# A planner that knows ScalarE's table loads and has own constants for two halves of the program, 128-row opening matmuls, and evictions shared between engines, in a hybrid encoder layer

## The chip, the cores and the metric

The kernel runs on one core of a Trainium2 chip. The metric is device time in microseconds (us), from the start of the program to its end. The time before is the median of three runs, 1055.0 us (1053.02 to 1058.98). The core has five engines that run their own instruction streams: PE (TensorE, matmuls), DVE (VectorE), ACT (ScalarE), POOL (GpSimd), and SP (SyncE, which here only issues transfers). They wait for each other through semaphores.

## The reference

One layer of an encoder over `x` of shape (1, 512, 1024), in float32. All constants below are fixed: 32 SSD heads of 64 in 8 groups, state 128, chunks of 128 tokens; 16 query heads and 4 key/value heads of 64; a feed-forward width of 4096.

```python
h = rmsnorm(x, pre_mix_norm)
z, xbc, dt_raw, q, k, v, gates = split_cols(h @ w_in, IN_SPLITS)      # w_in: 1024 x 9792
y_ssd  = ssd_branch(z, xbc, dt_raw, ...)      # conv of 5 taps, silu, scan in both directions, gated norm, @ w_ssd_out
y_attn = window_attention(q, k, v, attn_sink, rel_bias_table) @ w_attn_out     # +-128 tokens
g = sigmoid(gates + b_gate)
mixed = (g_ssd * y_ssd + g_attn * y_attn) @ w_o
x = x + rmsnorm(mixed, post_mix_norm)
h = rmsnorm(x, pre_mlp_norm)
f = square(relu(h @ w_mlp_in)) @ w_mlp_out    # 1024 x 4096 and 4096 x 1024
x = x + rmsnorm(f, post_mlp_norm)
```

The scan of one group and direction takes, for each chunk of 128 tokens, the product of the group's C and B (a 128x128 matrix), decays it, multiplies it with the chunk's inputs, and adds what the state carries over from the chunks before; the state itself is a product of B (transposed) with the weighed inputs.

## The kernel before, in words

**Numbers.** A large float32 operand is split into a rounded high part `hi` and the rest `lo`, both in the type fp32r, and a product is done as three matmuls into one accumulator: hi*hi, hi*lo, lo*hi (`mm3`). Each weight of 128x1024 thus needs a cast for its high part (ACT: line 585 in the in-projection, 1783 in the MLP) and a subtraction for its low part (lines 589 and 1792). Strings of letters say who subtracts: "v" is DVE, "p" POOL in quarters, "d" ACT and an adding DMA of POOL. The w_o product and the MLP are done by Strassen's scheme: seven products of half-size blocks, so the operands are also sums of blocks (`sums`, line 1671; `fold2`, line 1737). Small operands (`split`, lines 532 and 533) are cast on ACT and subtracted on DVE.

**Stages, by the trace's times.** Opening (0 to 25 us, `start`): load x, spread the norm weights over all partitions, norm, transpose and split the first 256 tokens' activations, and project to `v` and `dt`. Then the in-projection in column chunks of 128 with the scan of the eight groups and the attention heads worked in between (25 to about 690 us); the mix with w_o (to about 722); `norm_rows`, `flip_h2` (line 1630: the normed rows are transposed by 32 PE transposes, 16 for each half of the tokens, and scaled by the norm weight as they leave PSUM, line 1648) and the MLP's operands; the MLP's four up-projections U0 to U3 and four down-projections D0 to D3 (to 1041), and the closing norm (to 1054).

**The scan around the change.** For a group, the conv of B ends on ACT, its transpose goes through DRAM (the tile `pd`, written and read by SP, lines 1009 and 1012), the result is weighed, cast to `bth` (line 532) with a rest `btl`, also named `bth` in the profile (line 533), and then multiplied with the chunks' inputs `xh` on PE. Between the matmuls that make B and those that use `bth`, PE has other columns of the in-projection to work on: matmuls `pp<-b,wh` of 512 columns.

**The order.** The program is first written down in the order of Python, quantum by quantum. `Planner` (line 171) then simulates the five engines with a cost for every instruction, chooses for each engine the next instruction of those that are ready in the simulation, and `chain` (line 620) fixes the resulting order of every engine by dependencies. Matmuls are taken in program order, except that `next_matmul` (line 214) prefers those whose operands have been ready for some spare time (`SPARE_TIME`, by the engine that makes them), and holds the present kind of matmul (fp32r, fp32, or 64 rows wide) for up to `HOLD` ns before it changes kind; before `EARLY` ns of simulated time the hold is off. The other engines take what is due first (`deadlines`, with `DUE`), and wait for a more urgent instruction if it comes within `WAIT` of its cost. `LONGER` is a factor on costs, `TAIL` and `LEAD` belong to a transfer. The order is thus a result of all costs together, and a new constant anywhere may move instructions everywhere behind it.

**The opening's clock.** The first instructions of PE are six products of a zero tile (`WARM`), whose results nobody reads; then `self.gb`, two products of a row of ones (1x128) with the norm weights (1x512), which spread these over the partitions.

Of the kernel before, what the change touches and what calls it, by code (L numbers as in the profile page):

```python
# [29 lines left out]
LO_EARLY = "pppp"  # L30
LO_LATE = "vvpp"
# [4 lines left out]
DEFER, DEFER_BY = (3, 5), 9  # L36
WARM2 = 0
EARLY = 20000
NORM2 = 1, 0, 1
LO_V = "pvpvpvpv"  # L40
# [4 lines left out]
FETCH, STAGE = 2, 1  # L45
# [3 lines left out]
DUE = 7000  # L49
FAR = 2  # L50
LO_UP = "vdvp"
LO_DN = "vpvvvv"
RELU = "aaaaaa"
ADDS = "vvvhh"
LO_F = (), ()
LO_END = "dv"
FLIP = 2
# [113 lines left out]
class Planner:  # L171
# [8 lines left out]
    HOLD = 4000  # L180
# [4 lines left out]
    def __init__(self, instructions, tags, held=()):  # L185
        names = {"PE": "PE", "DVE": "DVE", "Activation": "ACT", "Pool": "POOL", "SP": "SP"}
        self.ins = [i for i in instructions if type(i).__name__ != "BassTilePoolBoundary"]
        self.eng = [names[str(i.engine).split(".")[-1]] for i in self.ins]
        self.tags = tags
        self.depend()  # L190
        last = None
        for n, i in enumerate(self.ins):
            if self.eng[n] == "PE":
                last = n
            elif i.name in held:
                self.turn[n].add(last)
                self.next[last].append(n)
        self.cost = [self.duration(n) for n in range(len(self.ins))]
        self.kind = [self.matmul_kind(n) if e == "PE" else None for n, e in enumerate(self.eng)]

# [11 lines left out]
    SPARE_TIME = {"SP": 3000, "POOL": 500, "DVE": 500, "ACT": 500, "PE": 0}  # L212

    def next_matmul(self, some, ready, soft, t, kind):
# [9 lines left out]
        held = lambda n: ready[n] + (0 if t < EARLY else 2 if self.ins[n].is_transpose else 1) * self.HOLD  # L224
# [134 lines left out]
    TAIL = 1400  # L359
    LONGER = 1.02  # L360
# [8 lines left out]
    WAIT = 0.2  # L369

    def plan(self):
        wait = self.WAIT
# [10 lines left out]
        queue, kind, landed = 0.0, None, []  # L383
        order, self.when = {e: [] for e in self.OVERLAP}, {}
        for _ in self.ins:
# [6 lines left out]
            t, e = best  # L392
            some = avail[e]
# [11 lines left out]
            c *= (2 if t < self.COLD else 1) if e == "PE" else self.LONGER  # L405
            end = t + c
            if e == "SP":
                queue = max(queue, t + self.LEAD) + self.transfer(n)
                free[e], end = end, queue + self.TAIL
# [10 lines left out]
            else:  # L420
# [5 lines left out]
                end += 2500 if "DMA" in type(self.ins[n]).__name__ else 0  # L426
            for s in self.post[n]:
                same = self.eng[s] == e == "PE"
                ready[s] = max(ready[s], free[e] if same else end + self.AFTER[self.eng[s]])
                if self.eng[s] == "PE":  # L430
                    soft[s] = max(soft[s], ready[s] + self.SPARE_TIME[e])
                left[s] -= 1
                if not left[s]:
                    avail[self.eng[s]].append(s)
# [17 lines left out]
class Trunk:  # L452
# [215 lines left out]
    def start(self):  # L668
# [4 lines left out]
        g = [get("g") for _ in range(2)]  # L673
        for j in range(2):
# [6 lines left out]
        self.zero, one = get("zero", (128, 128)), get("one", (128, 128))  # L681
        nc.vector.memset(self.zero, 0.0)
# [30 lines left out]
        for j in range(2):  # L713
            self.mm(self.gb[j], one[:1], g[j][:1], True, True)
# [769 lines left out]
    def mix_second(self, k):  # L1484
# [15 lines left out]
        self.mheld.extend([{"S1": p}, {"S4": q}, {"A22": (c,)}])  # L1500
# [129 lines left out]
    def flip_h2(self, t2):  # L1630
# [28 lines left out]
    def operand_h(self, a, r, parts=1):  # L1659
# [6 lines left out]
        for i in range(parts):  # L1666
            c = slice(i * 1024 // parts, (i + 1) * 1024 // parts)
            self.split(hi[:, c], lo[:, c], r[:, c])
# [169 lines left out]
    def up_quanta(self, p, banks):  # L1838
# [10 lines left out]

        return self.fold2(src, self.hops, banks, self.up_done(p), LO_UP, after, True)  # L1850

# [82 lines left out]
    def down_quanta(self, part, banks):  # L1934
# [17 lines left out]
        return self.fold2(src, self.fops[part], banks, done, LO_END if part == 3 else LO_DN, lambda a: self.give(*self.fops[part].pop(a)), False, part == 3)  # L1952
# [127 lines left out]
```

## Time and profile before

| what | value |
|---|---|
| median of three runs | 1055.0 us (1053.02 to 1058.98) |
| the profiled execution | 1055.77 us, of which the span of the instructions is 1054.0 us |
| mean granted clock of PE over the span | 0.994 |
| PE busy | 1033.5 us, 98% of the span, 5808 records |
| DVE, ACT, POOL busy | 862.9, 694.7 and 689.6 us (82, 66 and 65%) |
| in the MLP, 722 to 1041 us: PE, DVE | 315.8 and 290.9 of 319 us busy |

In the profile's rows a line number is that of the code above, `out<-in` are the program's names with the buffer numbers left out, `128*128` the rows and columns of the array in use, and "[2.75 <-ACT bth L532]" says that the engine stood idle for 2.75 us just before, and that an instruction of ACT, on tile `bth`, line 532, ended that. A matmul with three fp32r products has three instructions; an fp32 matmul of the code has several records (two products of 1x512 are four records in the opening). Matmul records overlap in time, since the array is a pipeline; what one costs is the distance to the next one's start. PE's clock is granted by a throttle: in the stretches of a table by windows, PEclk is the share of the full speed.

### The profile page before, as it was taken

The page shows a single profiled execution, that of the slowest core. Times are in us where ns is not written, and L with a number is a line of the kernel's source. Part 1 is how long each engine was busy: PE and PEld are TensorE (multiplying, and loading weights), DVE is VectorE, ACT ScalarE, POOL GpSimd, SP SyncE. Part 2 cuts the span into 40 slices and gives each one's busy share as a digit, 9 for nine tenths or more (in the row PEclk, how much of TensorE's full clock was granted, in tenths as well). Part 3 has the DMA queues.
Part 4 walks back from the last instruction along what each step waited for, and adds up shares of the span by engine and source line. Part 5 has one row for each costly group of instructions (what it writes and reads, how often), then busy time and mean ns, then how long its engine had stood idle before and what let it go on. Part 6 is the DMA issues. An engine that isn't in the chain of part 4 may idle for free. (4 is left out here: it accounts for less than half of the span.)

```text
span 1054.0 us, 17140 instructions
## 1 busy us (share of the span) xinstructions
PE 1033.5 (98%) x5808; PEld 889.1 (84%) x5808; DVE 862.9 (82%) x1237; ACT 694.7 (66%) x1293; POOL 689.6 (65%) x784
## 2 busy tenths in 40 slices
PE   9999899999999999999999999999999999999996
PEld 7888788888888888887888888888999998998885
DVE  5668788787896986696988775779988989969998
ACT  4577778768776664755676423578975864856863
POOL 3556659667869988998989767548853554254410
PEclk9999999999999999999999999999999999999998
DMA  7439968979999776758682499676784754855953
GB/s 226 116 103 266 256 177 250 245 187 261 249 219 242 227 191 178 190 160 218 166 216 76 145 305 343 190 223 217 197 201 101 223 142 98 219 138 143 278 142 100
DMA packets 232424, 206.24 MB, mean 196 GB/s; under 512 B 15341, under 2 KB 185557, under 8 KB 232336
## 3 DMA queue, kind: packets, MB, share of 16 engines
q1 hardware_dynamic: 225068, 185.68, 61.9%
q0 software_dynamic: 7120, 19.40, 10.4%
q8 instruction: 46, 0.75, 0.3%
q14 instruction: 42, 0.34, 0.1%
q10 hardware_dynamic: 148, 0.07, 0.0%
HBM read 163.35 MB, written 29.69 MB: 183 GB/s over the span
## 5 line engine op out<-in xcount | busy, mean ns | idle before, releaser
L515 PE MATMUL pp<-b,wh 128*128 128x512 f32 (+1 forms) x1424 | 431.2, 384 | 2.0 <-DVE b L533 1.5
L589 POOL TENSOR_TENSOR wl<-wr,wh 128x256 fp32r<-128x256 f32 (+1 forms) x365 | 308.3, 871 | 110.7 <-ACT wh L585 81.2
L515 PEld LDWEIGHTS pp<-b,wh 128*128 128x128 f32 x1424 | 262.8, 189 | 53.8 <-DVE b L533 1.9
L515 PE MATMUL pp<-b,wl 128*128 128x512 f32 (+1 forms) x712 | 272.8, 384 | 0.0
L515 PEld LDWEIGHTS pp<-b,wl 128*128 128x128 f32 x712 | 134.4, 189 | 25.8 <-issue 0.3
L585 ACT CAST wh<-wr 128x1024 fp32r<-128x1024 f32 (+1 forms) x99 | 102.7, 1039 | 50.3 <-POOL wl L589 32.6
L1783 ACT CAST wh<-wd 128x1024 fp32r<-128x1024 f32 x63 | 65.2, 1050 | 19.3 <-PE ps L515 6.6
L1792 DVE TENSOR_TENSOR wl<-wd,wh 128x1024 fp32r<-128x1024 f32 x46 | 65.9, 1444 | 8.2 <-ACT wh L1783 6.7
L515 PE MATMUL ps<-b,wh 128*128 128x256 f32 x400 | 72.0, 283 | 0.0
L515 PE MATMUL pp<-wh,fh 128*128 128x512 f32 x176 | 68.9, 392 | 0.8 <-ACT fh L1699 0.6
L515 PE MATMUL pp<-wl,fh 128*128 128x512 f32 x176 | 68.9, 391 | 0.2 <-DVE wl L1792 0.2
L515 PE MATMUL pp<-wh,fl 128*128 128x512 f32 x176 | 67.8, 390 | 0.0
L515 PEld LDWEIGHTS ps<-b,wh 128*128 128x128 f32 x400 | 62.3, 191 | 0.9
L515 PE MATMUL ps<-b,wl 128*128 128x256 f32 x200 | 55.7, 284 | 0.0
L1792 POOL TENSOR_TENSOR wl<-carved,wh 128x256 fp32r<-128x256 f32 x32 | 40.0, 1294 | 14.1 <-ACT wh L1783 7.2
L1792 POOL TENSOR_TENSOR wl<-wd,wh 128x256 fp32r<-128x256 f32 x24 | 35.5, 1504 | 19.4 <-ACT wh L1783 17.8
L1783 ACT CAST wh<-carved 128x1024 fp32r<-128x1024 f32 x34 | 35.4, 1049 | 19.0 <-DVE carved L1744 10.8
L515 PE MATMUL ps<-sh,wh 128*128 128x256 f32 x160 | 45.3, 283 | 0.0
L515 PE MATMUL ps<-sh,wl 128*128 128x256 f32 x160 | 45.2, 283 | 0.0
L515 PE MATMUL ps<-sl,wh 128*128 128x256 f32 x160 | 45.2, 283 | 0.0
L1788 POOL DMA_DIRECT2D wl<-carved x11 | 9.9, 901 | 48.8 <-ACT wl L1787 38.4
L515 PEld LDWEIGHTS pp<-wh,fh 128*128 128x128 f32 x176 | 33.1, 188 | 7.8 <-ACT fh L1699 0.8
(968 smaller groups left out, 2636.9 us busy)
## 6 DMA issues: line engine op xcount, KB each, us to landing
wr<-in_w_in SPq DMA_DIRECT2D x74, 512.0 KB, 5.7
wd<-in_w_mlp_out SPq DMA_DIRECT2D x26, 512.0 KB, 5.7
wd<-in_w_mlp_in SPq DMA_DIRECT2D x22, 512.0 KB, 5.4
pd<-t SPq DMA_DIRECT2D x16, 640.0 KB, 6.0
pT<-pd SPq DMA_DIRECT2D x64, 160.0 KB, 5.7
wr<-in_w_ssd_out SPq DMA_DIRECT2D x14, 512.0 KB, 4.4
rf<-csT SPq DMA_DIRECT2D x27, 256.0 KB, 5.6
wl<-carved POOLq DMA_DIRECT2D x11, 512.0 KB, 6.1
```

Of the source, the lines that this page charges most:

```text
L515: self.nc.tensor.matmul(out, lhsT, rhs, start=start, stop=stop, skip_group_check=more)
L585: self.nc.scalar.copy(hi[:, :m], raw)
L589: engines[e].tensor_tensor(lo[:, c], raw[:, c], hi[:, c].bitcast(F32), op=ALU.subtract)
L1783: nc.scalar.copy(hi, w)
L1788: nc.gpsimd.dma_start(low, w, accum_op=ALU.add)
L1792: (nc.vector if e == "v" else nc.gpsimd).tensor_tensor(low[:, q], w[:, q], hi[:, q].bitcast(F32), op=ALU.subtract)
```

## The change

1. **The planner** adds 1283 ns to the simulated cost of an instruction of ACT whose activation table is another than the last one's (`table_of`: Ln and Sqrt each their own, Exp and Tanh together). Its constants `HOLD`, `SPARE_SP`, `SPARE_VEC`, `TAIL`, `LONGER` and `WAIT` have a value for the scan and one for what follows `ENTRY` = 690000 ns of simulated time (`HOLD` a third one from 30 us later). `HOLD` becomes 8000, 500, 4000 (was 4000), the spare time for a transfer's result 1000 and 3000 (was 3000), that for a vector engine's 500 and 800 (was 500), `TAIL` 1600 and 1400 (was 1400); `WAIT` and `LONGER` keep their values. `EARLY` goes from 20 to 80 us and `DUE` from 7000 to 6000.
2. **The opening** fills `g` and `one` with zeros on all 128 rows, so that the products that spread the norm weights are 128 rows deep. The identity's transfer is issued ahead of those of `g`, which wait for the zeros. `WARM2` adds two products of the zero tile; the order puts them beside the six that were there. The low parts of the opening's weights are all subtracted on DVE (`LO_V`).
3. **Shares.** Low parts: the gates' weights (`LO_EARLY`, `LO_LATE`) and, of the weights of the first two up-projections, the fourth of every four (`LO_UP`) go from POOL to DVE. Half of the 16 evictions behind the PE transposes of `flip_h2` go from ACT to DVE (`EVICT_H`), and the first relu and square of each up-projection become one instruction of DVE (`RELU`).
4. **Places.** `FLIP` 2 to 1, `FETCH` 2 to 1, `DEFER` without quantum 5, and `mix_second` holds the block sum `q` one product longer.

Counted over both programs: DVE does 6 more low parts of 128x1024 in the MLP, 4 more instructions of 128x512 (relu), 8 more of 128x256 (evictions), 24 more low parts of 128x256 in the gates, 4 more of 128x320 and two more fills; POOL does 24 fewer pieces of 128x256 in the MLP, 24 fewer in the gates and 4 fewer of 128x320; ACT does 8 fewer instructions of 128x512 and 8 fewer of 128x256; PE has two more 128x128 products. ACT's table loads are four in both programs, ahead of the same instructions (lines 735, 892, 990 and 1960).

```diff
-LO_EARLY = "pppp"
-LO_LATE = "vvpp"
+LO_EARLY = "vvpp"
+LO_LATE = "vvvp"
-DEFER, DEFER_BY = (3, 5), 9
-WARM2 = 0
-EARLY = 20000
+DEFER, DEFER_BY = (3,), 9
+WARM2 = 2
+EARLY = 80000
-LO_V = "pvpvpvpv"
+LO_V = "vvvvvvvv"
-FETCH, STAGE = 2, 1
+FETCH, STAGE = 1, 1
-DUE = 7000
+DUE = 6000
-LO_UP = "vdvp"
+LO_UP = "vdvv", "vdvv", "vdvp", "vdvp"
+EVICT_H = "av", "av"
-RELU = "aaaaaa"
+RELU = "vaaaaa"
-FLIP = 2
+FLIP = 1
...
-    HOLD = 4000
+    ENTRY = 690000
+    HOLD = 8000, 500, 4000
...
+    @staticmethod
+    def table_of(i):
+        f = str(getattr(i, "func", "")).split(".")[-1]
+        return f if f in ("Ln", "Sqrt") else "Exp" if f in ("Exp", "Tanh") else None
...
-    SPARE_TIME = {"SP": 3000, "POOL": 500, "DVE": 500, "ACT": 500, "PE": 0}
+    SPARE_SP = 1000, 3000
+    SPARE_VEC = 500, 800
...
+        hold = self.HOLD[(t > self.ENTRY) + (t > self.ENTRY + 30000)]
...
-    TAIL = 1400
+    TAIL = 1600, 1400
+    TABLE = 1283
...
+            if e == "ACT" and self.table[n] not in (None, table):
+                c, table = c + self.TABLE * (table is not None), self.table[n]
...
         g = [get("g") for _ in range(2)]
+        self.zero, one = get("zero", (128, 128)), get("one", (128, 128))
+        nc.vector.memset(self.zero, 0.0)
+        nc.vector.memset(g[0], 0.0)
+        nc.gpsimd.memset(g[1], 0.0)
         for j in range(2):
             nc.scalar.dma_start(g[j][:1], self.d_pre_mix_norm[0:1, j * 512:(j + 1) * 512])
...
-        self.zero, one = get("zero", (128, 128)), get("one", (128, 128))
-        nc.vector.memset(self.zero, 0.0)
+        nc.vector.memset(one, 0.0)
         nc.vector.memset(one[:1], 1.0)
...
-            self.mm(self.gb[j], one[:1], g[j][:1], True, True)
+            self.mm(self.gb[j], one, g[j], True, True)
...
-        self.mheld.extend([{"S1": p}, {"S4": q}, {"A22": (c,)}])
+        self.mheld.extend([{"S1": p}, {"S3": q}, {"A22": (c,)}])
...
                 for i in range(2):
-                    nc.scalar.activation(r[:, (k + i) * 256:(k + i + 1) * 256], ps[:, i * 256:(i + 1) * 256], AF.Copy,
-                                         scale=self.g3(4 * kh + k + i))
+                    dst, src, g = r[:, (k + i) * 256:(k + i + 1) * 256], ps[:, i * 256:(i + 1) * 256], self.g3(4 * kh + k + i)
+                    if EVICT_H[t2][(4 * kh + k + i) % len(EVICT_H[t2])] == "a":
+                        nc.scalar.activation(dst, src, AF.Copy, scale=g)
+                    else:
+                        nc.vector.tensor_scalar(dst, src, g, None, op0=ALU.mult)
```

**The order at three places.** In the rows, the numbers behind a name tell tiles apart and differ between the two programs; "x3" is three instructions in a row.

PE at the states of scan group 0 (about 111 us in the trace). `pp_1300` (after: `pp_1305`) is a column chunk of the in-projection with 24 matmuls of 512 columns, `C,bt` the products of C and B, and `xh,bth` the state products. Before:

```order
L515 MATMUL pp_1300<-b_143,wh_1101 128x512
L515 MATMUL pp_1300<-b_145,wh_1101 128x512
L515 MATMUL pp_1300<-b_143,wl_1102 128x512
L515 MATMUL pp_1300<-b_143,wh_1101 128x512
L515 MATMUL pp_1300<-b_145,wh_1101 128x512
L515 MATMUL ps_1273<-C_1093,bt_927 128x128 x2
L515 MATMUL ps_1278<-xh_1122,bth_1118 128x256 x2
```

After:

```order
L532 MATMUL pp_1305<-b_149,wl_1107 128x512
L532 MATMUL pp_1305<-b_149,wh_1106 128x512
L532 MATMUL pp_1305<-b_151,wh_1106 128x512
L532 MATMUL ps_1278<-C_1098,bt_932 128x128 x2
L532 MATMUL ps_1283<-xh_1127,bth_1123 128x256 x3
L532 MATMUL ps_1288<-xh_1127,bth_1123 128x256 x3
L532 MATMUL pp_1305<-b_149,wl_1107 128x512
```

Before, five matmuls of the chunk stand ahead of the state products and 19 behind them; now 23 stand ahead and one behind.

ACT at the same place: the cast of `bth` and what stands ahead of it (`rf` are decays of the scan, line 1266, and `P` softmax numerators, line 990, 997). Before:

```order
L997 ACTIVATE E_1029<-E_1029,sm_1048 128x256
L997 ACTIVATE P_1066<-P_1066,sm_1048 128x256
L585 CAST wh_1255<-wr_1108 128x1024
L1266 ACTIVATE rf_1026<-rf_1026,tables_403 128x128 x3
L990 ACTIVATE P_1202,sm_1197<-P_1202,mx_1196 128x384
L532 CAST bth_1118<-tables_403 128x4x4x32
```

After:

```order
L1017 ACTIVATE E_1034<-E_1034,sm_1053 128x256
L549 CAST xh_1240<-bt_932 128x512
L1017 ACTIVATE P_1071<-P_1071,sm_1053 128x256
L602 CAST wh_1260<-wr_1113 128x1024
L549 CAST bth_1123<-tables_408 128x4x4x32
L1180 ACTIVATE C_1098<-pp_1188 128x512
```

The three decays and the softmax numerator that stood between the weight's cast and that of `bth` stand elsewhere now.

PE at the entry of the MLP (about 719 us in the trace). `ps<-ident,x` are the transposes of the first half of the tokens, `pp_7117` (after: `pp_7121`, `pp_7122`) the last products of the mix, and `pp_7606` (after: `pp_7608`) the first product of the MLP. Before:

```order
L519 MATMUL ps_7492<-ident,x_610_7177 128x128
L519 MATMUL ps_7492<-ident,x_611_7180 128x128
L515 MATMUL pp_7117<-wh_7413,fc_6999 128x512 x2
L515 MATMUL pp_7606<-b_7463,wh_7418 128x256
```

After:

```order
L536 MATMUL ps_7497<-ident,x_609_7181 128x128
L536 MATMUL ps_7497<-ident,x_610_7184 128x128
L532 MATMUL pp_7121<-wh_7408,fc_6832 128x512
L532 MATMUL pp_7121<-wh_7414,fc_7002 128x512 x3
L532 MATMUL pp_7121<-wh_7418,fc_7002 128x512 x3
L532 MATMUL pp_7122<-wh_7408,fc_6832 128x512
L532 MATMUL pp_7122<-wl_7409,fc_6832 128x512
L532 MATMUL pp_7122<-wh_7408,fc_6832 128x512 x2
L532 MATMUL pp_7122<-wl_7409,fc_6832 128x512
L532 MATMUL pp_7122<-wh_7408,fc_6832 128x512
L532 MATMUL pp_7122<-wh_7414,fc_7002 128x512 x3
L532 MATMUL pp_7122<-wh_7418,fc_7002 128x512 x3
L532 MATMUL pp_7608<-b_7468,wh_7423 128x256 x2
```

Before, two matmuls of the mix stand between the last transpose and the MLP's first product; now 19 do. Two more counts of this kind, over stretches too long to show: from the last matmul of B's product to the first state product of group 6, PE has 89 matmuls of 512 columns before, and 92 and 16 small ones of 64 columns more now; and from the second half's transposes to the first product of the operand `S2`, which needs them, 44 matmuls of 256 columns before and 112 now.

More of the change, by code (lines that the diff above doesn't have):

```diff
@@ L198, in __init__ @@
         self.cost = [self.duration(n) for n in range(len(self.ins))]
+        self.table = [self.table_of(i) if e == "ACT" else None for i, e in zip(self.ins, self.eng)]
         self.kind = [self.matmul_kind(n) if e == "PE" else None for n, e in enumerate(self.eng)]
+    @staticmethod
+    def table_of(i):
+        f = str(getattr(i, "func", "")).split(".")[-1]
+        return f if f in ("Ln", "Sqrt") else "Exp" if f in ("Exp", "Tanh") else None
     def matmul_kind(self, n):
@@ L223, in next_matmul @@
             return (same or other or now)[0]
-        held = lambda n: ready[n] + (0 if t < EARLY else 2 if self.ins[n].is_transpose else 1) * self.HOLD
+        hold = self.HOLD[(t > self.ENTRY) + (t > self.ENTRY + 30000)]
+        held = lambda n: ready[n] + (0 if t < EARLY else 2 if self.ins[n].is_transpose else 1) * hold
         return same[0] if same and min(held(n) for n in now if self.kind[n] != kind) > t else first
@@ L358 @@
     LEAD = 1000
-    TAIL = 1400
-    LONGER = 1.02
+    TAIL = 1600, 1400
+    LONGER = 1.02, 1.02
+    TABLE = 1283
     def transfer(self, n):
@@ L382, in plan @@
         port = {"DVE": 0.0, "POOL": 0.0}
-        queue, kind, landed = 0.0, None, []
+        queue, kind, landed, table = 0.0, None, [], None
         order, self.when = {e: [] for e in self.OVERLAP}, {}
@@ L392, in plan @@
             t, e = best
+            late_half = t > self.ENTRY
+            wait = self.WAIT[late_half]
             some = avail[e]
@@ L426, in plan @@
                 end += 2500 if "DMA" in type(self.ins[n]).__name__ else 0
+            spare = {"SP": self.SPARE_SP[late_half], "PE": 0}
+            spare = {e: spare.get(e, self.SPARE_VEC[late_half]) for e in free}
             for s in self.post[n]:
@@ L430, in plan @@
                 if self.eng[s] == "PE":
-                    soft[s] = max(soft[s], ready[s] + self.SPARE_TIME[e])
+                    soft[s] = max(soft[s], ready[s] + spare[e])
                 left[s] -= 1
@@ L1667, in operand_h @@
             c = slice(i * 1024 // parts, (i + 1) * 1024 // parts)
-            self.split(hi[:, c], lo[:, c], r[:, c])
+            self.nc.scalar.copy(hi[:, c], r[:, c])
+            if a in LO_H:
+                for q in (slice(c.start, (c.start + c.stop) // 2), slice((c.start + c.stop) // 2, c.stop)):
+                    self.nc.gpsimd.tensor_tensor(lo[:, q], r[:, q], hi[:, q].bitcast(F32), op=ALU.subtract)
+            else:
+                self.nc.vector.tensor_tensor(lo[:, c], r[:, c], hi[:, c].bitcast(F32), op=ALU.subtract)
         self.hops[a] = hi, lo
```

14 lines of the change are left out of this document (7 added, 7 removed).

## The prediction

> **What bounds the kernel now.** I read the page's busy shares first, then PE's waits, then the time by stages.
>
> ```profile
> PE 1033.5 (98%) x5808; PEld 889.1 (84%) x5808; DVE 862.9 (82%) x1237; ACT 694.7 (66%) x1293; POOL 689.6 (65%) x784
> PE ps L515 <- ACT bth L532: 5.2, 2, 2.8
> PE pp L515 <- DVE b L533: 1.5, 2, 0.8
> PE ps L519 <- DVE junk L741: 0.9, 1, 0.9
> PE pp L515 <- ACT fh L1699: 0.6, 1, 0.6
> ```
>
> PE is the bound: the span of 1054.0 less 1033.5 leaves 20.5 us in which it stood. A change that takes no matmul away can win only these, and what PE does at less than its full clock. The waits are columns of total, count and longest: two waits for `bth` make up 5.2 us. The closing stretch below holds 9.6 us more of the 20.5. The table of windows (start and end, length, then busy time of PE, its weight loads, DVE, ACT, POOL; granted clock; DMA share; GB/s) shows where:
>
> ```profile
> 0.00:16.60 16.60, 14.68 (x44) 9.77 (x45) 9.86 (x20) 9.04 (x21) 5.61 (x12) 1.00 0.77 230
> 112.00:120.00 8.00, 5.25 (x20) 4.21 (x19) 5.14 (x14) 7.81 (x23) 5.53 (x7) 0.79 1.07 295
> 115.60:119.10 3.50, 3.50 (x11) 2.74 (x10) 1.20 (x5) 3.50 (x14) 1.93 (x3) 0.51 1.00 325
> 488.00:496.00 8.00, 5.59 (x21) 4.45 (x20) 3.34 (x6) 5.78 (x14) 5.83 (x8) 0.79 0.85 208
> 491.10:494.60 3.50, 3.50 (x12) 3.02 (x13) 2.94 (x5) 2.37 (x7) 2.26 (x2) 0.51 1.08 273
> 722.00:762.00 40.00, 37.77 (x306) 36.67 (x306) 38.56 (x39) 37.77 (x70) 35.34 (x45) 1.00 0.68 185
> 762.00:880.00 118.00, 118.00 (x792) 109.28 (x791) 102.27 (x86) 82.16 (x105) 63.43 (x53) 1.00 0.66 166
> 880.00:1041.00 161.00, 159.99 (x928) 141.09 (x927) 150.04 (x151) 105.17 (x129) 52.90 (x50) 1.00 0.64 161
> 1041.00:1054.00 13.00, 3.40 (x26) 2.96 (x24) 9.05 (x22) 2.33 (x8) 0.00 (x0) 0.75 0.44 162
> ```
>
> Each of the two `bth` waits is followed by some 3.5 us at a clock of 0.51, so it costs twice: once as a wait, once as half of the following 3.4 us or so. In the opening, 14.68 of 16.60 us are busy; its clock is printed as 1.00, but the durations below say half. Between the stalls PE is full, and the MLP from 762 on is full as well, with DVE close behind.
>
> **The two stalls in the scan.** Group 0, from the timeline:
>
> ```profile
> 112.74 0.98 ACT L1266 ACTIVATE rf<-rf,tables 128x128 f32<-128x128 f32 x3 [0.19 <-POOL rf L1264]
> 113.63 0.60 ACT L990 ACTIVATE P<-P,mx 128x384 f32<-128x384 f32 x1
> 114.23 0.60 ACT L532 CAST bth<-tables 128x512 fp32r<-128x512 f32 x1
> 114.89 0.73 PE L515 MATMUL ps<-xh,bth 128*128 128x256 f32 x4 [2.75 <-ACT bth L532]
> 487.71 0.39 PE L515 MATMUL pp<-b,wl 128*128 128x512 f32 x1
> 487.94 0.61 PE L515 MATMUL pp<-b,wh 128*128 128x512 f32 x2
> 493.59 0.63 PE L515 MATMUL pp<-b,wl 128*128 128x512 f32 x1
> 494.01 0.86 PE L515 MATMUL pp<-b,wh 128*128 128x512 f32 x2
> ```
>
> A matmul of 512 columns costs 487.94 − 487.71 = 0.23 us at the full clock and 494.01 − 493.59 = 0.42 at the half one. In the order, 18 matmuls of 512 columns come ahead of the state products that stood behind them: 18 × 0.227 (0.23 before rounding) = 4.1 us of work against a wait of 2.75. On ACT the three decays and a numerator no longer stand right ahead of the cast: 0.98 and 0.60 us less, if `bth`'s source is there by then. So the wait is covered with some 1.3 us to spare even if ACT gains nothing. Gone are 2.75 + 3.4 × 0.5 = **4.45 us**. What covered PE is now one matmul instead of 19 behind the first state products; these then go on to the next group of 512-column products, which are ready.
>
> Group 6:
>
> ```profile
> 485.57 1.75 SPq L1012 DMA_DIRECT2D V<-pd x4
> 490.29 0.62 ACT L532 CAST bth<-V 128x512 fp32r<-128x512 f32 x1 [1.10 <-DMA V<-pd]
> 490.96 1.12 PE L515 MATMUL ps<-xh,bth 128*128 128x256 f32 x4 [2.41 <-ACT bth L532]
> L515 PE MATMUL ps<-pT,V 128*64 128x128 f32 x320 | 19.8, 275 | 0.0
> ```
>
> Here the trip of B through DRAM is late: ACT itself waited 1.10 us for it. The order puts three more 512-column matmuls and 16 of 64 columns between B's product and its states; 64-column ones are two records each, and 19.8 / 320 = 0.062 us per record, so 3 × 0.227 + 32 × 0.062 = 2.7 us against 2.41. That is just enough, so I leave a residual wait of 0.5: 2.41 + 1.7 − 0.5 = **3.6 us**. (If the wait is 1 us later than counted it does not drop the clock: no wait under 2.4 us in PE's list is followed by a half-clock window.) Bounds: 0 to 4.1. The table cost itself moves nothing directly: four table loads before and after, at the same instructions.
>
> **The opening.**
>
> ```profile
> 3.90 3.78 PE L515 MATMUL pp<-g,zero 1*128 1x512 f32 x4
> 7.76 1.40 DVE L741 SCALAR_TENSOR_TENSOR junk<-x,rst,pp 128x512 f32<-128x512 f32 x2
> 8.56 1.97 PE L519 MATMUL ps<-ident,junk 128*128 128x128 f32 x8 [0.88 <-DVE junk L741]
> 11.75 1.54 ACT L701 CAST wv<-wr 128x320 fp32r<-128x320 f32 x4
> 14.42 3.30 PE L515 MATMUL pp<-wv,b 128*128 128x320 f32 x14
> 17.56 2.51 PE L515 MATMUL ps<-wv,b 128*128 128x320 f32 x16
> ```
>
> Matmuls of 320 columns cost 3.30 / 14 = 0.24 us until about 16.6 and 2.51 / 16 = 0.16 behind it: the clock doubled there, about 15 us after PE's first matmul, although PE was busy nearly throughout. What differs from the later stretches is that 3.78 of the 4.7 us from 3.90 to 8.56 go to products that fill one of 128 rows. With 128 rows, the stretch may count as work and the clock rise a few windows earlier. What that can win is capped: the weights' high parts end on ACT at 11.75 + 1.54 = 13.29, and the products of 320 columns need them, so the 14 end at best at 13.29 + 14 × 0.16 = 15.5, 2.1 us before 17.56. The other end: two more zero products, two records of 128 columns each like the transposes' (1.97 / 8 = 0.25 us), put 1.0 us ahead of the spread if the clock stays as it is, and DVE at 7.76 needs the spread. (The fills of `g` stand ahead of its transfer, but beside those zero products.) Between −2.1 and +1.0 I take **−1.3**, nearer to the gain: 14 × (0.24 − 0.16) = 1.1 if those products run at the full clock, and 0.2 for an earlier start.
>
> Rival to it: *the clock falls back.* From 8.56 on, PE does 16 transposes and little else until 14.4; if transposes are not work enough to hold the clock, what the spread has won is lost there, the products run as before, and the zero products remain: +1.0 in place of −1.3. The 16 transposes at 719.66 (below) kept the spacing of the full clock, 1.91 / 16 = 0.12 us, but filled only half of a stretch of 3.4 us, so they show little. [...] No row of this trace decides it.
>
> **The entry of the MLP.**
>
> ```profile
> 719.66 1.91 PE L519 MATMUL ps<-ident,x 128*128 128x128 f32 x16
> 721.33 0.71 PE L515 MATMUL pp<-wh,fc 128*128 128x512 f32 x2
> 723.33 0.39 PE L515 MATMUL pp<-b,wh 128*128 128x256 f32 x1 [0.77 <-DVE b L533]
> 749.21 0.50 PE L515 MATMUL pp<-b,wh 128*128 128x256 f32 x2 [0.44 <-ACT b L532]
> 750.47 0.39 PE L515 MATMUL pp<-b,wh 128*128 128x256 f32 x1 [0.76 <-DVE b L533]
> ```
>
> The way from the transposes to the first product is eviction, cast, subtraction. 19 matmuls (19 × 0.227 = 4.3 us) cover it now instead of two (0.45), so 0.77 goes, and for `S2` 112 matmuls of 0.12 us (13.4) stand where 44 (5.3) stood, so 0.44 + 0.76 go: 1.97 in all. Against that, the second half's rows must be ready some 8 us earlier, on a DVE that is busy 38.56 of 40 us here, and the transposes are cut into pieces with more changes of kind. I take **−1.6**, bounds −2.0 and +1.
>
> **The shared work.** POOL is relieved and costs nothing. DVE gets, in the MLP:
>
> ```profile
> L1792 DVE TENSOR_TENSOR wl<-wt,wh 128x1024 fp32r<-128x1024 f32 x7 | 12.5, 1786 | 0.5 <-ACT wh L1783 0.5
> L1744 DVE TENSOR_TENSOR wt<-wd,carved 128x1024 f32<-128x1024 f32 x7 | 8.5, 1221 | 0.5 <-PE pp L515 0.4
> L1728 DVE TENSOR_TENSOR fr<-fr,ps 128x512 f32<-128x512 f32 x11 | 7.2, 679 | 0.3 <-PE ps L515 0.2
> ```
>
> 6 × 1.22 + 4 × 0.74 (a three-operand one at 128x512, half of the 1.40 above and a little) + 8 × 0.41 (a bit more than half of 0.679) = 7.3 + 3.0 + 3.3 = 13.6 us. With low parts at 1.79, the dearest row, it is 17. DVE idles 1.4 + 15.7 us between 722 and 880, where most of this falls; the windows' room is thus just filled. [...] I take **+0.5**; from 0 to 13.6 if all of it lands on PE's path.
>
> **The rest is dealt anew.** `HOLD` doubles in the scan, spare times and due times differ, and a planner that deals 4600 matmuls anew will close some gaps and open others. What is left of PE's idle time, 20.5 less 9.6 at the close, 5.2 for `bth`, 2.0 at the MLP's entry and 1.9 in the opening, is 1.8 at best; one new stall like the two above costs 4.45. Nearer to the loss, since the old order had two such in eight groups: **+1.5**.
>
> **The sum** against the profiled execution's 1055.77: −4.45 − 3.6 − 1.3 − 1.6 + 0.5 + 1.5 = −8.95, thus 1046.8. This execution stands 0.77 above the median of 1055.0, so for the median **1046 us**.
>
> **The rivals.**
>
> *The clock falls back in the opening*, as worked out above: 1046 + 1.0 + 1.3 = 1048.3.
>
> *A new stall of the `bth` kind.* The order changes the distance from B to its states in every group; any that comes short by over 2.4 us costs 4.45. For it: the two groups that stalled came from the same planner. Against it: spare times now differ for transfers. Result 1046 + 4.45 = 1050.5.
>
> *DVE becomes the bound of the MLP.* It decides if what is added finds no idle time on DVE ahead of its consumers, in the first up-projections (96% busy in 722 to 762). Then all 13.6 us stand in PE's way instead of 0.5, and the entry's 1.6 are lost too: 1046 + 13.1 + 1.6 = 1060.7, slower than before. Against it: 15.7 us of room in 762 to 880, and POOL has been relieved by 24 pieces of 1.2 us or more.
>
> *It does more*: the whole opening (−2.1), the whole entry (−2.0), and the small waits go (−1.8 instead of +1.5): 1046 − 0.8 − 0.4 − 3.3 = 1041.5.
>
> *The stalls move instead of going*: the simulated costs still miss the real trip through DRAM, so that two others appear in their place and nothing else is dealt worse: 1046 + 4.45 + 3.6 − 1.5 = 1052.6.
>
> **How the numbers follow.** Chances: forecast 0.38 (own range 1043 to 1049), the clock falls back 0.15, one new stall 0.20, stalls move 0.07, more 0.12, DVE the bound 0.08. What can be told from no change is 0.5%, or 5.3 us: faster is below 1049.7, slower above 1060.3. Faster: 0.38 + 0.13 of the 0.15 + 0.12 + 0.06 of the 0.20 = 0.69; slower 0.08; the rest, 0.23, is the same. The range runs from 1038, the best case less 0.5 for each of group 6's residual and the shared work and the 2 us by which the fastest run lies under the median, to 1056, the worst of the other cases and 3 us more; it leaves out DVE as the bound and some of the edges, some 0.15 in all.
>
> **What would show it.** The waits for `bth` gone from PE's list and the windows near 112 and 488 at a clock of 1.00; products of 320 columns at 0.16 us from their first; the waits for `b` near 722 and 750 gone; DVE's busy time in 722 to 880 up by about 13 us with PE still full there. Wrong it would be with a window at 0.51 anywhere between 25 and 1041, with waits for DVE's `wl` or `fl` on PE between 722 and 880, or if the opening's 14 products still take 3.3 us.

## The result, and the profile after

The changed kernel ran in 1047.59 us (median of ten runs, 1044.51 to 1054.07), beside 1055.24 us for the kernel before (ten runs, 1052.35 to 1058.98). The ratio is 0.9937 (95% interval 0.9912 to 0.9963): faster by 0.6%. In a later session it was 1053.55 beside 1056.53, a ratio of 0.9962 (0.9934 to 0.9991). It is faster in both, by 3 to 8 us.

The profiled execution is the slowest of the ten, 1054.07 us with a span of 1051.9. PE's waits in it (total, count, longest):

```profile
PE ps L532 <- ACT wh L1811: 4.0, 1, 4.0
PE ps L532 <- ACT bth L549: 2.1, 3, 1.5
PE ps L532 <- DVE zero L692: 1.6, 1, 1.6
PE pp L536 <- DVE hr L1672: 1.5, 1, 1.5
PE pp L532 <- DVE carved L1975: 1.4, 1, 1.4
PE pp L536 <- ACT wh L1811: 1.3, 1, 1.3
```

The two waits of 2.8 and 2.4 us for `bth` are gone; the longest for it is 1.5. In their place stands one of 4.0 us for a weight's cast in the MLP (line 1811 is 1783 of before), and there are new ones at the MLP's entry (`hr`, and the 1.3 for `wh`). The same stretches as before, by windows:

```profile
112.00:120.00 8.00, 8.00 (x41) 6.77 (x41) 7.20 (x15) 5.08 (x13) 6.18 (x9) 1.00 1.07 308
488.00:496.00 8.00, 8.00 (x38) 6.67 (x39) 7.96 (x12) 5.30 (x13) 8.00 (x10) 1.00 0.81 190
722.00:762.00 40.00, 38.07 (x316) 37.52 (x315) 39.51 (x45) 30.69 (x46) 33.89 (x23) 1.00 0.72 189
762.00:880.00 118.00, 113.96 (x736) 105.04 (x735) 97.76 (x85) 79.32 (x99) 42.34 (x41) 0.97 0.62 151
```

Both stretches of the scan are full and at the full clock. The one from 762 to 880, which was full before, lacks 4.04 us of PE and has a clock of 0.97: from 771.54 on the clock is half for 6.83 us. That begins 1.3 us before the wait ends, so 5.53 us of PE's work run at half clock and lose 2.8 us.

To compare kernels I cut every profiled execution at three places of the program: the first product with K's weights (end of the opening), U0's first product (end of scan and mix), and PE's last instruction (end of the MLP). All times in us; "table" says whether the planner counts table loads; the ratio is that of runs to runs of the kernel before on the same chip.

| kernel | table | opening | scan and mix | MLP | rest | ratio (95%) |
|---|---|---|---|---|---|---|
| before | no | 31.6 | 690.5 | 322.9 | 9.1 | 1 |
| changed | yes | 28.2 | 685.2 | 329.4 | 9.1 | 0.9937 (0.9912 to 0.9963) |
| changed, again (e12) | yes | 29.0 | 683.1 | 328.1 | 9.1 | 0.9962 (0.9934 to 0.9991) |
| before with HOLD (e1) | no | 31.8 | 688.8 | 323.0 | 8.9 | 0.9958 (0.9936 to 0.9979) |
| before with table (e2) | yes | 30.0 | 683.5 | 322.8 | 8.8 | 0.9936 (0.9914 to 0.9958) |
| before with table and opening (e5) | yes | 28.6 | 682.3 | 325.3 | 8.9 | 0.9905 (0.9879 to 0.9931) |
| before with opening (e6) | no | 28.9 | 691.9 | 323.7 | 9.0 | 0.9976 (0.9952 to 1.0000) |
| before with TAIL (e11) | no | 29.1 | 694.9 | 324.3 | 7.5 | 1.0013 (0.9982 to 1.0044) |
| changed, one-row opening (e3) | yes | 31.9 | 685.1 | 329.2 | 9.1 | 0.9976 (0.9949 to 1.0003) |
| changed, eps on DVE (e4) | yes | 28.6 | 688.4 | 322.1 | 9.1 | 0.9930 (0.9906 to 0.9954) |
| changed, no table (e7) | no | 28.2 | 696.5 | 329.4 | 9.3 | 1.0020 (0.9994 to 1.0046) |
| changed, old shares (e8) | yes | 28.3 | 686.1 | 333.2 | 9.0 | 0.9994 (0.9972 to 1.0016) |
| e8, eps on DVE (e10) | yes | 28.4 | 687.8 | 329.9 | 9.0 | 0.9989 (0.9963 to 1.0016) |
| e4 with the old scan constants (e9) | yes | 28.3 | 682.5 | 326.6 | 7.5 | 0.9906 (0.9869 to 0.9944) |

A stage is one execution, the ratio many; the same order differs by some us from one execution to the next (685.2, 683.1, 685.1 and 688.4 in the scan of the changed kernel, e12, e3 and e4, whose scans have one order). Read the stages for what is large in them: every scan planned without the table loads takes 688.8 us or more, every one with them 688.4 or less. By its stages, the changed kernel gains 2.1 us in the first profiled execution and 4.9 in the second; by the medians it gains 7.7 and 3.0. What the faster executions of the first session do otherwise is not shown.

### The profile page after: what moved, and what is told of

The parts are those of the page before. It is cut to its first block, busy times and chain, and to the rows that moved or that the text cites. A ratio compares the mean times of both kernels' runs of the same rounds, so it can differ in the third digit from the quotient of the medians.

```text
span 1051.9 us, 17148 instructions
## 1 busy us (share of the span) xinstructions
PE 1028.1 (98%) x5812; PEld 886.5 (84%) x5812; DVE 887.2 (84%) x1285; ACT 687.0 (65%) x1277; POOL 652.2 (62%) x733
## 4 chain that ended last, share of the span: by engine, by line
PE 77%; DVE 6%; DMA 6%; POOL 5%; issue 3%; ACT 2%; SPq 2%; DVEq 0%; ACTq 0%; POOLq 0%
PE pp L532 53%; PE ps L532 23%; POOL wl L606 2%; SPq L1032 1%; DVE wl L1820 1%; DMA wd<-in_w_mlp_in 1%; DMA E<-pd 1%; DMA carved<-in_w_mlp_in 1%; POOL eps L1644 1%; DMA pd<-C 1%; DMA post_mlp_norm<-in_post_mlp_norm 1%; DMA bt<-pd 1%; DVE carved L1772 0%; PE ps L536 0%; DMA pd<-t 0%
## 5 line engine op out<-in xcount | busy, mean ns | idle before, releaser
L606 POOL TENSOR_TENSOR wl<-wr,wh 128x256 fp32r<-128x256 f32 (+1 forms) x341 | 292.4, 883 | 98.0 <-ACT wh L602 62.1
L602 ACT CAST wh<-wr 128x1024 fp32r<-128x1024 f32 (+1 forms) x99 | 102.7, 1038 | 48.3 <-POOL wl L606 24.8
L1820 DVE TENSOR_TENSOR wl<-wd,wh 128x1024 fp32r<-128x1024 f32 x39 | 54.5, 1403 | 13.3 <-ACT wh L1811 10.6
L1811 ACT CAST wh<-carved 128x1024 fp32r<-128x1024 f32 x44 | 46.0, 1048 | 26.3 <-PE ps L532 10.9
L1811 ACT CAST wh<-wd 128x1024 fp32r<-128x1024 f32 x54 | 55.9, 1045 | 10.2 <-POOL rs L1627 2.0
L1816 POOL DMA_DIRECT2D wl<-wd x12 | 10.6, 887 | 68.3 <-ACT wl L1815 34.8
L1820 POOL TENSOR_TENSOR wl<-carved,wh 128x256 fp32r<-128x256 f32 x28 | 32.1, 1206 | 14.4 <-ACT wh L1811 14.4
L532 PE MATMUL pp<-ah,wh 128*128 128x512 f32 x128 | 40.2, 390 | 0.0
```

Source lines behind the costliest of these rows:

```text
L532: self.nc.tensor.matmul(out, lhsT, rhs, start=start, stop=stop, skip_group_check=more)
L602: self.nc.scalar.copy(hi[:, :m], raw)
L606: engines[e].tensor_tensor(lo[:, c], raw[:, c], hi[:, c].bitcast(F32), op=ALU.subtract)
L1811: nc.scalar.copy(hi, w)
L1816: nc.gpsimd.dma_start(low, w, accum_op=ALU.add)
L1820: (nc.vector if e == "v" else nc.gpsimd).tensor_tensor(low[:, q], w[:, q], hi[:, q].bitcast(F32), op=ALU.subtract)
```

## The experiments

**The scan: which constant? (e1, e2)**

My theory was the prediction's: `HOLD` at 8000 puts more matmuls ahead of the states, and the table cost moves nothing. e1 has `HOLD` alone, e2 the table cost alone.

```diff
-    HOLD = 4000
+    HOLD = 8000, 4000        # up to 690 us, behind it
...
+    TABLE = 1283             # e2 instead, with table_of and the line that adds it
```

> The kernel before, with one constant changed: HOLD is 8000 up to 690 us of simulated time and 4000 behind it. In the order, 23 instead of 5 matmuls of the chunk stand ahead of group 0's state products; group 6 gets only 0.5 us more work ahead of its own. Theory (it is HOLD that covers the stalls): the wait of 2.75 us for bth near 112 us and the half-clock stretch behind it are gone (4.45 us), the one near 488 us stays at about 2 us or turns up at another group; the time is 1049 to 1052. Rival (the table loads in the simulated costs are what does it): the wait near 112 stays above 2 us, and the time is 1055 within 2.

> The kernel before, with the table loads of 1283 ns added to the simulated costs and nothing else. In the order, ACT's cast of bth of group 0 stands one place earlier, and PE still has 5 matmuls of the chunk ahead of the state products. Theory (the accounting alone covers nothing): both waits for bth, near 112 and 488 us, stay above 2 us and the time is 1055 within 3. Rival (ACT's earlier place for the cast is enough): the wait near 112 is below 1.5 us and its half-clock stretch is gone, some 4 us less.

e1 measured 1051.73 us, a ratio of 0.9958: the wait near 112 is gone and no `bth` wait is over 0.6 us, so `HOLD` alone does cover group 0, as said. The other half of its theory fell: the wait near 488 did not stay, and what turned up elsewhere (1.0 us near 190 and 1.5 near 226, not for `bth`) came without a half-clock window. And e2 measured 1048.06, a ratio of 0.9936, as much as the whole change. There my theory fell, and the rival held, with twice the 4 us that it gave: the wait near 488 shrank too, to 1.1 us, and its half-clock window went. Its waits, and group 0 in its timeline:

```profile
PE pp L524 <- DVE b L542: 1.5, 2, 0.8
PE ps L528 <- DVE junk L750: 1.4, 1, 1.4
PE ps L524 <- ACT bth L541: 1.1, 1, 1.1
107.34 0.61 ACT L541 CAST bth<-tables 128x512 fp32r<-128x512 f32 x1
109.13 0.60 PE L524 MATMUL ps<-C,bt 128*128 128x128 f32 x4
109.49 0.96 PE L524 MATMUL ps<-xh,bth 128*128 128x256 f32 x6
```

PE's order at group 0 is the old one, with five matmuls ahead. What differs is ACT's: the cast of `bth` now stands directly behind the softmax divisions (`P<-P,sm`), ahead of the weight's cast and the numerator that stood before it, and the three decays are elsewhere. Before, it ended 0.06 us before PE could start on it; here it ends at 107.95, 1.5 us ahead of PE. Covering the wait with matmuls and having the cast earlier are two remedies for one stall, and the changed kernel has both.

**Is it the accounting, or any new order? (e7, e11)**

A new cost deals the whole order anew, so e2 could be luck. e7 takes the accounting out of the changed kernel; e11 deals the old order anew through another constant.

```diff
-    TABLE = 1283
+    TABLE = 0                # e7, in the changed kernel
...
-    TAIL = 1400
+    TAIL = 1600              # e11, in the kernel before
```

> The changed kernel with the cost of a table load set to 0 in the planner, everything else as changed (its orders keep 23 matmuls ahead of group 0's states). Theory (with HOLD at 8000 the stalls near 112 and 488 are covered anyhow, so the accounting is one of two covers there): no bth wait near 112, and a median within 3 us of the changed kernel's 1047.6. Rival (the accounting sets the order in the rest of the scan too, and carries the gain): 1050 to 1054, with waits for bth or for ACT's results over 1 us between 120 and 690 us that the changed kernel does not have.

> The kernel before with TAIL at 1600 and nothing else: an order dealt anew (the distances of groups 3, 4 and 7 grow by 2 to 4 us, that of group 6 shrinks by 0.9, group 0 keeps its 5 matmuls), without any accounting of table loads. Theory (a new deal by itself gives nothing as long as the simulated ACT runs ahead of the real one): both stalls for bth stay, a ratio of 0.998 to 1.003. Rival (any new deal of this order gains, and the accounting was one of many): 0.995 or less.

e7 measured 1057.43 us beside 1057.56: without the accounting nothing is left of the gain. Its theory (`HOLD` covers the stalls anyhow) fell; the rival was right, and still too mild. Group 0 has no wait, but group 6 has the longest of all:

```profile
PE ps L532 <- ACT bth L549: 5.9, 3, 3.4
PE ps L532 <- ACT wh L1811: 4.3, 1, 4.3
492.44 0.89 PE L532 MATMUL ps<-xh,bth 128*128 128x256 f32 x4 [3.39 <-ACT bth L549]
```

e11 measured 1057.20, a ratio of 1.0013: the new deal gives nothing. That its two `bth` stalls would stay was wrong, though: they went (0.8 us in all), and two others came, 3.1 us for `xh` near 535 and 2.2 for a weight's cast near 611:

```profile
PE ps L515 <- ACT xh L532: 3.1, 1, 3.1
PE pp L515 <- ACT wh L585: 2.2, 1, 2.2
```

So three orders planned with an ACT that never loads a table (before, e7, e11) each have two waits over 2 us on ACT's results between 100 and 620 us, at different places; with the loads counted, none in e2, e5 and e9, planned with the old constants, is over 1.2. (In the changed kernel's own order one near 537 is left, from 0.6 us in e12 to 2.8 in e4.) e1 shows that more matmuls in between help as well, to about half the amount (4.3 us beside 8.0 by the medians). So counting the loads brings the gain, in the kernel before (e2) and in the changed one (e7 without it). How it does so is argued only. The two loads near 48 and 60 us, of 1.28 us each, may leave the real ACT behind the simulated one from there on and eat the spare time of half a microsecond; but ACT is busy for 66% of the span and could catch up, and no run measures the lag. And e11 is the only order dealt anew for no reason: how often such a deal gains is not known.

**The opening (e3, e6)**

In the changed kernel's opening, PE:

```profile
5.16 2.78 PE L532 MATMUL pp<-g,zero 128*128 128x512 f32 x4
8.10 1.34 PE L536 MATMUL ps<-ident,junk 128*128 128x128 f32 x8 [0.16 <-DVE junk L761]
12.06 2.65 PE L532 MATMUL pp<-wv,b 128*128 128x320 f32 x14
14.55 2.51 PE L532 MATMUL ps<-wv,b 128*128 128x320 f32 x16
```

The spread takes 2.78 instead of 3.78 us, the transposes 1.34 instead of 1.97, and the second 16 products of 320 columns start at 14.55 instead of 17.56. e3 puts the spread back to one row, and e6 gives the kernel before the new opening.

```diff
-            self.mm(self.gb[j], one, g[j], True, True)
+            self.mm(self.gb[j], one[:1], g[j][:1], True, True)     # e3
```

> The changed kernel, with the two products that spread the norm weights over one row again (1x128 with 1x512; the fills of g and one stay, and the order of every engine is the same). Theory (the depth of 128 rows is what lets the clock rise early): the products of 320 columns cost 0.24 us again until about 16 us, and the opening ends about 3 us later, as in the kernel before: the first product of K's weights starts near 31.4 instead of 28.2 us. Rival (the fills, the identity's place in the queue and DVE's low parts did it): it starts within 0.7 us of 28.2.

> The kernel before with the 128-row opening alone. Theory (the clock rises some 4 us earlier): K's first product near 28.5 us, and the median 2 to 3.5 us below the kernel before, if the later order keeps its two stalls for bth. Rival (another engine takes the time back before 31 us): K's first product later than 30 us and a median within 1 us of before.

e3, with all fills, the queue and the order as changed:

```profile
5.30 3.78 PE L532 MATMUL pp<-g,zero 1*128 1x512 f32 x4
9.00 2.03 PE L536 MATMUL ps<-ident,junk 128*128 128x128 f32 x8
14.93 3.48 PE L532 MATMUL pp<-wv,b 128*128 128x320 f32 x14
18.25 2.51 PE L532 MATMUL ps<-wv,b 128*128 128x320 f32 x16
```

The slow opening is back: K's products start at 31.93 us. So the depth of 128 rows is the cause, as the theory had it. e6 starts them at 28.85, and is 1.6 us faster by its median and 2.5 by the ratio (0.9976), whose interval just reaches 1; that does not decide about the theory's 2 to 3.5. Over all profiles, the clock is full from 4.9 to 7.0 us on in the nine executions with 128 rows, and for good from 11.4 to 17.5 in the five with one row (in e11 it was full from 4.6, fell back at 8.0, behind the one-row products and a wait, and rose again at 11.4); K's products start at 28.2 to 29.0 and at 29.1 to 31.9. In one-row executions the moment varies by up to 6 us, and with it what the new opening saves: their K's products start within 2.9 us of each other.

**The wait near 768 us (e4, e12)**

Followed back in the changed kernel's timeline:

```profile
745.48 1.21 DVE L1707 TENSOR_TENSOR hr<-hr,carved 128x1024 f32<-128x1024 f32 x1
745.64 13.16 POOL L1646 TENSOR_SCALAR eps<-eps 128x1 f32<-128x1 f32 x1
757.50 1.21 DVE L1820 TENSOR_TENSOR wl<-wd,wh 128x1024 fp32r<-128x1024 f32 x1
758.64 0.68 DVE L1756 TENSOR_TENSOR carved<-carved,pp 128x512 f32<-128x512 f32 x1
758.85 1.25 POOL L1787 DMA_DIRECT2D carved<-in_w_mlp_in  x1
764.92 1.06 ACT L1815 ACTIVATE wl<-carved 128x1024 fp32r<-128x1024 f32 x1 [6.26 <-DMA carved<-in_w_mlp_in]
771.75 1.04 ACT L1811 CAST wh<-wd 128x1024 fp32r<-128x1024 f32 x1
772.84 0.58 PE L532 MATMUL ps<-b,wh 128*128 128x256 f32 x1 [4.04 <-ACT wh L1811]
```

An instruction of POOL on 128 numbers stands for 13.16 us. DVE meanwhile runs 13 instructions back to back, all with two operands in SBUF (one with the same tile twice); POOL's ends 0.16 us after DVE starts one that reads PSUM (`pp`). Only then, at 758.85, does POOL issue the adding transfer for a weight (line 1787), ACT waits 6.26 us for it, and PE 4.04 for a cast that stands several places behind on ACT. Before, the same instruction at that place took 1.06 us, although DVE ran two-operand instructions without a gap there too:

```profile
751.47 1.22 DVE L1744 TENSOR_TENSOR wt<-wd,carved 128x1024 f32<-128x1024 f32 x1
752.60 1.22 DVE L1679 TENSOR_TENSOR hr<-hr,carved 128x1024 f32<-128x1024 f32 x1
752.83 1.06 POOL L1626 TENSOR_SCALAR eps<-eps 128x1 f32<-128x1 f32 x1
753.74 1.22 DVE L1688 TENSOR_TENSOR carved<-carved,s 128x1024 f32<-128x1024 f32 x1
```

It ended 0.15 us after DVE's next instruction began; the three eps instructions ahead of it (1.24, 1.02 and 1.06 us, from 749.25 on) ended 0.16, 0.12 and 0.14 us after the start of one of DVE's as well. So a DVE without gaps alone does not make an instruction of POOL long. Why POOL's took 1.06 us there and 13.16 in the changed kernel is not known.

e4 gives the 24 small instructions of the closing norm's eps to DVE, and leaves all others in the order they had; e12 is the changed kernel once more.

```diff
-        tt, e = nc.gpsimd.tensor_tensor, self.eps2[:, t:t + 1]
+        tt, e = nc.vector.tensor_tensor, self.eps2[:, t:t + 1]
...
-        nc.gpsimd.tensor_scalar(e, e, 1.0 / D, EPS, op0=ALU.mult, op1=ALU.add)
+        nc.vector.tensor_scalar(e, e, 1.0 / D, EPS, op0=ALU.mult, op1=ALU.add)
```

> The changed kernel, with the 24 instructions of 128x1 that work out the closing norm's eps (lines 1641 to 1646) on DVE instead of POOL; all other instructions keep the order they had. Theory (on POOL these small instructions stood for 5.9, 5.6 and 13.2 us behind a DVE that ran one two-operand instruction after the other, and held up the adding transfer queued behind them, whose product PE then waited 4.0 us for near 768 us): no instruction of POOL in 700 to 770 us lasts over 3 us, the wait near 768 is gone with its half-clock stretch (5.7 us in such an execution), and the time is 1041 to 1045 with all runs within 4 us of each other. Rival (the transfer itself lands late, or it waits for a buffer): the wait near 768 stays, and the time is 1047 within 2, with the spread of 1044 to 1054 as before.

> The changed kernel once more, for another execution's profile and its time beside the others on one chip. Theory (POOL's starved instruction is fixed by the order of DVE): instructions of 128x1 on POOL of about 5.9, 5.6 and 13.2 us again and the wait of 4 us near 768 us again, a ratio of 0.991 to 0.996. Rival (it hits only some executions): no such wait in this profile.

e12 has the same three long instructions (5.91, 5.62 and 13.16 us) and the same wait, so it is the order that fixes them:

```profile
743.77 13.16 POOL L1646 TENSOR_SCALAR eps<-eps 128x1 f32<-128x1 f32 x1
PE ps L532 <- ACT wh L1811: 4.1, 1, 4.1
```

In e4 no such instruction is left, the wait near 768 is gone, and the MLP takes 322.1 us instead of 329.4 and 328.1: the eps instructions on POOL are the cause of this wait. The time is not what the theory gave: 1047.06 us, and runs from 1043.5 to 1052.5 instead of 1041 to 1045. Its scan took 688.4 us in the profiled execution, with waits of 2.8 us for `bth` near 537 and 1.5 for `x` near 183 that are 1.5 and 0.5 in the changed kernel's. Why the ratio (0.9930 beside 0.9937 and 0.9962) does not show the 7 us that the MLP's stage shows stays open; the intervals are some 5 us wide, and e4 and the changed kernel ran in different sessions.

**The MLP's shares (e8, e10)**

```diff
-LO_UP = "vdvv", "vdvv", "vdvp", "vdvp"
+LO_UP = "vdvp", "vdvp", "vdvp", "vdvp"
-EVICT_H = "av", "av"
+EVICT_H = "aa", "aa"
-RELU = "vaaaaa"
+RELU = "aaaaaa"
```

> The changed kernel with the MLP's shares as before: POOL takes the fourth low part of the first two up-projections, ACT all evictions of the transposes and all relus. Theory (the denser DVE is what keeps POOL's small instructions from running): no instruction of 128x1 on POOL lasts over 3 us in 700 to 770 us, no wait near 768 us, and the median is 1044 to 1047, with the slowest run under 1051. Rival (the shares are worth the 13.6 us of DVE that they cost): waits for ACT's or POOL's results in the first up-projections, 1048 to 1052.

> The kernel of e8_shares0 (the MLP's shares as before) with the eps instructions on DVE. Theory (its loss came from one instruction of 128x1 on POOL that stood for 9.1 us, so that the second half's rows came 5.2 us late for PE's transposes): that wait is below 2 us, and the ratio to before is 0.992 to 0.996. Rival (the loss is ACT's and POOL's work, which the shares take off them): the waits for rows and for POOL's low parts stay, and the ratio is 0.997 or more.

e8 measured 1056.75, so its theory (without the shares POOL is not starved) fell; the waits of its rival came, with a time above its 1048 to 1052:

```profile
712.00 9.12 POOL L1641 TENSOR_TENSOR eps<-sq 128x1 f32<-128x1 f32 x1 [1.68 <-ACT carved L1636]
720.38 0.68 DVE L1696 TENSOR_TENSOR b<-carved,b 128x512 fp32r<-128x512 f32 x1
723.80 0.75 DVE L1632 SCALAR_TENSOR_TENSOR x<-h,rs,x 128x512 f32<-128x512 f32 x1 [2.74 <-POOL rs L527]
PE pp L536 <- DVE x L1629: 5.2, 1, 5.2
```

POOL has a long instruction here too, now of 9.12 us: it ended at 721.12, 0.06 us after DVE had run out of work, and what stands behind it on POOL (`rs`, the rows' scale) holds up the second half's rows, for which PE's transposes wait 5.2 us. e10 takes the eps instructions off POOL: that wait falls to 3.3 us, those for POOL's low parts (2.3) and ACT's evictions (1.3) stay, and the ratio is 0.9989. So the rival of e10 was right: with the transposes at their new, earlier place, ACT and POOL can't do the old shares in time. Given that place, the shares are needed; they win nothing over the old place with the old shares (322.8 us in e2 beside 322.1 in e4).

**Two parts of the change alone (e5, e9)**

e5 is the kernel before with the table loads counted and the 128-row opening, nothing else. e9 has e5's scan and the changed MLP with eps on DVE.

```diff
-    HOLD = 8000, 500, 4000
+    HOLD = 4000, 500, 4000            # e9, from e4; also SPARE_SP 3000, TAIL 1400, EARLY 20000, DUE 7000,
-FETCH, STAGE = 1, 1                   # DEFER (3, 5), LO_EARLY "pppp", LO_LATE "vvpp"
+FETCH, STAGE = 2, 1
```

> The kernel before, with the table loads in the simulated costs and with the 128-row opening (fills of g and one, identity first, two more zero products), and nothing else: constants, shares and places are the old ones. Theory (these two parts carry the whole gain, and the rest of the change gives nothing): 8 us from the accounting as in e2_table, 2 to 3 more from the opening, 1045 to 1047, with none of the waits of 4 us near 768 or over 1 us near 186 and 537 that the changed kernel shows. Rival (the gain of e2_table was its execution's opening and chance of the new order): 1050 to 1054.

> The changed kernel with the scan side as before (HOLD 4000, spare time 3000, TAIL 1400, EARLY 20000, DUE 7000, FETCH 2, DEFER with 5, the gates' low parts on POOL), but with the table loads in the costs, the 128-row opening, all of the changed MLP, and the eps instructions on DVE as in e4_eps. The scan's order is that of e5_table_open. Theory (the accounting and the opening carry the scan, and the changed MLP is good once POOL is not starved): U0's first product near 711 us as in e5_table_open, 331 us from there to the end as in e4_eps, thus 1042 to 1045 for a run, and a ratio to before of 0.985 to 0.989. Rival (the changed MLP is no better than the old one): 1046 to 1048, a ratio of 0.990 or more.

e5 measured 1046.45 us beside 1057.56, a ratio of 0.9905, with runs from 1045.9 to 1049.8: its theory held. Its longest waits:

```profile
PE pp L524 <- DVE wl L1804: 2.4, 2, 1.5
PE ps L524 <- DVE zero L684: 1.6, 1, 1.6
PE pp L524 <- DVE b L542: 1.5, 2, 0.8
```

e9 measured 1046.94, 0.9906: U0 starts at 710.86 us as expected, but the MLP takes 326.6 us, with new waits of 0.8 to 1.6 us at its entry (one of them for the moved eps instructions) and two over 1 us near 1011 and 1018. It is no better than e5, so its rival held. Two of the change's parts give 0.95%, at least as much as the whole. That the rest gives some of it back is likely, not shown: e5 was not run side by side with the changed kernel, and of that one's two intervals the first overlaps e5's and the second just does not.

## Why the prediction was right, and where it was wrong

The time (1046 forecast, 1047.59 measured, range 1038 to 1056) and the sign were right. That the total is so close is luck in part. In the later session the same kernel gained 3.0 us by the medians, and the sum came out through errors that offset each other:

- **Group 0's stall, −4.45**: right. 18 more matmuls cover it, and the half-clock window behind it went with it.
- **Group 6's stall, −3.6 with 0.5 left**: the half-clock window went; waits of 0.4, 0.4 and 0.8 us for `bth` and `xh` near 482 to 487 are left, thus −2.5. (In e2, planned with the old `HOLD`, that wait is 1.1 us, so the 2.7 us of added matmuls are not the only way to it.)
- **"The table cost itself moves nothing directly: four table loads before and after, at the same instructions"**: this step failed. The loads don't move, but counting them changes the order behind them, and with it comes nearly all of the scan's gain (e2, e7). I had read the cost as an event on the chip instead of a part of the simulation from which the order is made.
- **The scan as a whole**: −8.05 + 1.5 = −6.55 forecast; −5.3 and −7.4 in the two executions.
- **The opening, −1.3, at best −2.1**: too small. −3.4 and −2.7 in the profiles, −1.6 by e6's median. The cap was wrong: the 14 products don't wait for all high parts but run as they come, from 12.06 us while ACT's last cast ends near 13.1. The rival in which the clock falls back over the transposes did not happen: transposes and products from 8.10 us on keep the short spacing (1.34 / 8 = 0.17 us a transpose, part of it still waiting, against 0.25 before). In e11 the clock was half from 8.01 to 11.42 and full behind it; in that stretch PE ran 12 transposes, from 8.28 to 10.75, and two products of 320 columns. There were matmuls beside the transposes in both openings, and no run had transposes alone, so what they do to the clock by themselves was not shown.
- **The MLP's entry, −1.6**: it went the other way. The waits for `b` near 722 and 750 are gone, as said (1.97 us), but 1.34, 1.50 and 0.43 us came at the second half's transposes and right behind them, 3.3 in all. "The second half's rows must be ready some 8 us earlier, on a DVE that is busy" was the right worry with too low a price.
- **"POOL is relieved and costs nothing", and +0.5 for DVE's added work**: failed. The 0.5 was an estimate from DVE's 1.4 and 15.7 us of idle time; that DVE's own work gets cheaper as POOL's gets less, no run shows. PE never waits for DVE's 13.6 us as such, so the rival of DVE as the bound did not come true. But beside DVE's instructions some of POOL's smallest ones last up to 13.16 us, and through a transfer and a cast PE loses 4.0 us and then runs at half clock for 3.0 or 5.5 us: 5.6 us lost in e12, 6.8 in the first profile. The MLP came out at +6.6 and +5.2 against a forecast of −1.1. The prediction had no term for this. The shares are not needed for it, since e8 with the old ones has an instruction of 9.12 us; which of the places and constants of the new MLP order bring it was not separated.
- **The signs**: the two windows in the scan are full, as said. One sign of being wrong came true: a half-clock window between 25 and 1041 us, at 771.54. And DVE's busy time in 722 to 880 went from 140.8 to 137.3 us instead of up by 13. The program is some 9 us ahead there, and the largest group of DVE's low parts (`wl<-wd,wh`) took 1.40 instead of 1.44 us apiece over the whole run; e8, with the old shares, has 123.8 us in that window, 13.5 less than with the new ones.

## What to carry to other kernels

A planner that fixes an order by simulation should count rare events too: counting the table loads, 1.28 us each in a span of 1054, gave as much by itself (e2) as the whole change, and no longer counting them took all of the changed kernel's gain (e7). With the loads counted, the scan's new constants brought nothing that shows here (e9 beside e4), although one of them had helped without (e1). After work has been moved or an order dealt anew, look in the profile for instructions that are tiny by their shape and long in time, and at what stands behind them in their queue. And cut both traces at the same places of the program before trusting a sum: here an opening better than forecast and an MLP that lost 5 us or more hid behind a total that looked right.

## What the runs showed of the hardware

- An instruction of POOL on 128x1 elements took 13.16 us, to the hundredth the same in four executions of that order of the MLP (the changed kernel, e3, e7, e12), while DVE ran 13 instructions with two operands in SBUF without a gap; others of its shape took 0.19. The long ones of the changed kernel (5.92, 5.62 and 13.16 us) ended 0.12 to 0.16 us after DVE began an instruction on PSUM or one with a scalar per partition, and the one of 9.12 us in e8 0.06 us after DVE went idle. With the eps instructions on DVE (e4) none of POOL's from 700 to 770 us lasted over 1.5 us. In the kernel before, four in a row from 749.25 us on took 1.02 to 1.24 us beside a DVE that also ran two-operand instructions without a gap, each ending 0.12 to 0.16 us after one of these began. No run shows what decides.
- The clock of PE was full for good from 4.9 to 7.0 us on in the nine executions whose opening products used 128 rows (7.0 in the first of the changed kernel), and from 11.4 to 17.5 in the five with one row (16.6 in the kernel before), with about the same instructions.
- A wait of PE did not always cost its clock: 2.75 us near 112 and 2.41 near 488 did, before (3.41 us at half clock for each), and 2.2 near 486 in e6; 2.8 us near 537 in e4, 2.7 near 533 in e8 and 2.2 near 539 in e3 did not. Waits of 3.1 (e11) and 4.0 us cost one or two windows of 3.4 us; that of 4.0 in the changed kernel cost 6.83 us at half clock.
